# Moving GpSimd's arithmetic to accumulating transfers, TensorE and VectorE in a two-layer decoder trunk

## Chip, cores and metric

The program runs on one core of a Trainium2 chip. The metric is the device time of one execution in microseconds; the time before is the median of three runs. Five engines work side by side and meet at semaphores: TensorE (PE, with its weight loads PEld), VectorE (DVE), ScalarE (ACT), GpSimd (POOL) and SyncE (SP). SP issues plain transfers. POOL issues the transfers that add to what lies at their destination; these appear in the trace as DMA_DIRECT2D on POOL, and their packets as the software_dynamic queue.

## What is computed

A hidden state of 528 tokens (16 learned ones and 512 of the input) by 1024 channels, held transposed as eight tiles `h[m]` of 128 channels x 528 tokens, goes through two layers.

- Layer 0, mixer: RMS norm, one input projection to q, k, v, forget gates and a gated convolution branch. Eight heads of causal attention with forget gates run beside a causal depthwise convolution of width 31 over 4 x 128 channels (`u[i]` in, `cv[i]` out), a layer norm over these 512 channels and SiLU. One output projection maps both back, and the result is added to `h`.
- Layer 1, mixer: causal mean pooling with windows 2, 4, 8 and 16 over four groups of channels, each mean less the channel itself, then a 256 x 256 product for each group, scaled and added to `h`.
- After each mixer a gated MLP: RMS norm, up-projection to 2 x 2816, causal depthwise convolution of width 3, SiLU(gate) x value, down-projection, residual.
- A final RMS norm; the 16 learned tokens are dropped.

## The kernel before

**Weights.** Every 128 x 128 weight tile is used in two float32r parts: a rounded part `wH` and the rest `wL`. Activations are split into `xH`, `xL` likewise, and a product is three matmuls (`xH wH`, `xL wH`, `xH wL`) of 264 columns for each half of the tokens. Weights arrive in chunks of eight tiles (512 KB). `prepare(c)` loads a chunk (SP, `raw<-wts`), rounds it to `wH` (L224 on ACT, or L225 on DVE for the 20 numbers in `VECTOR_CHUNKS`), writes `-wH` into `wL` (L178, ACT) and lets POOL issue a transfer that adds `raw` to it (L179). Three chunks are in flight up to the first MLP, then four. A projection tile of 128 outputs in layer 0's mixer uses exactly one chunk.

**Order.** Matmuls are in the order written in the program: `first_products` (gates and the first tile, k by k as `h` arrives), 7 more tiles of the convolution branch, and then `PE_ORDER`, in which `F` is half of a q, k or v tile, `MA0` to `B13` are steps of the four pairs of heads, `O` is half an output tile, and SUM, MEAN, VAR and SILU are the layer norm's steps. In the pooling, DVE's order is written out as well, in `POOL_ORDER`: `Z` scales by the norm's factor R, `S` makes the window sums, `T` corrects the first 16 tokens, `D` forms the result and adds it to `h`, `X` splits `h` into `xH`, `xL` and issues the matmuls of four up-projection tiles for this k, `Q` squares for the next norm. All other instructions are placed by a planner that simulates the program; each engine then runs its own list strictly in order.

**The 31 convolution taps.** When `u[i]` is complete, `done_g` puts its taps into two lists. Kind 0 is one DVE instruction per tap (L495). Kind 1 is a product on ACT (L498, two buffers) and an addition on POOL (L499). `fill(pace)` takes from the lists after every half tile, by the amounts in `PACE`; `ln_sum` (SUM) takes the rest.

**Sums of squares.** `squares(m, apart)` squares `h[m]` on ACT (L247) and adds it to `acc` on POOL (L249); the last `apart` tiles go to the matmul with ones by themselves. Five norms use it: before layer 0's mixer (`APART[0]`, while `h` arrives), after the output projection, in the second half of each down-projection, and in the pooling.

**Other work on POOL.** Clearing constants (`late`, held behind the first norm's sums), `u x sigmoid` (L479), the layer norm's sums (L758, L768, L787), some casts of q and k (`COPIES`, letter P), small casts (L414, L622, L720), the gates' sum (L529), three of the `Z` (`POOL_Z`, L1013), six of the additions to `h` in `D` (`POOL_RES`, L1037), and six of the sixteen last output tiles (L1092).

Of the kernel before, what the change touches and what calls it, by code (L numbers as in the profile page):

```python
# [20 lines left out]
KT = 8  # L21
# [38 lines left out]
POOL_CHUNKS = (6, 7, 8, 10, 13, 14, 15, 16, 17, 18, 19, 20, 21, 22, 23, 24, 25, 28, 31, 34, 97, 98, 100, 101, 102, 104, 105, 106, 107)  # L60
# [18 lines left out]
POOL_RES = (1, 2, 3, 4, 5, 7)  # L79
POOL_Z = (1, 4, 6)  # L80
# [15 lines left out]
COPIES = ('AAAAA', 'VAAAV', 'APAAA', 'PAPAV')  # L96

VECTOR_CHUNKS = (2, 3, 6, 9, 10, 14, 26, 27, 29, 30, 31, 33, 34, 96, 100, 101, 102, 105, 106, 107)

WARM = 12  # L100

TAPS3 = 3
# [25 lines left out]
def trunk_kernel(  # L128
# [41 lines left out]
    def prepare(c):  # L170
# [69 lines left out]
    def squares(m, apart, t0=0, t1=T, part=True):  # L240
# [5 lines left out]
        sq = wk.tile([P, T], F32, tag="sq", name=f"sq{m}")  # L246
# [57 lines left out]
    with ExitStack() as mx:  # L304
# [31 lines left out]
        for m in range(KT):  # L336
            i_ = squares(m, APART[0], part=SPLIT_FIRST)
            if SQ_AFTER[m] is not None:
                after(i_, xs_[SQ_AFTER[m]])
        ident = pt[:, C_ID:C_ID + P]  # L340
# [47 lines left out]
        def late(ap, x):  # L388
            after(nc.gpsimd.memset(ap, x), state["sum"])

        def constants():
# [19 lines left out]
            for tri, to in ((upper, maskU), (lower, maskL)):  # L411
                late(to[:, P:P + NMETA], 0.0)
                for c0 in (0, P + NMETA):
                    after(nc.gpsimd.tensor_copy(to[:, c0:c0 + P], tri), state["sum"])  # L414
# [53 lines left out]
        def done_g(i):  # L468
            t_ = wk.tile([P, T], F32, tag="sq", name=f"sg{i}")

            def fn(hf, ps):
# [18 lines left out]
        def tap(i, j, kind):  # L490
# [18 lines left out]
        def first_products():  # L509
# [5 lines left out]
            ws = [next_weight(("in", "a", 0, k)) for k in range(KT)]  # L515
            for k in range(KT):
# [12 lines left out]
            nc.gpsimd.tensor_tensor(cell["f"], cell["f"], low, op=ALU.add)  # L529
# [71 lines left out]
        def attention(p):  # L601
# [6 lines left out]
            def values():  # L608
# [13 lines left out]
                nc.gpsimd.tensor_copy(hv2, hv.bitcast(F32))  # L622
# [59 lines left out]
            def scores(hh):  # L682
                tl = st[hh]
                for x, parts in enumerate(BL):
# [34 lines left out]
                    if x == 3:  # L719
                        nc.gpsimd.tensor_copy(P4[hh][64:80, :], ph.bitcast(F32))  # L720
# [35 lines left out]
        def sum_of(x, y, name):  # L756
            t_ = wk.tile([P, T], F32, tag="sq", name=name)
            nc.gpsimd.tensor_tensor(t_, x, y, op=ALU.add)  # L758
            return t_

        def ln_sum():
# [6 lines left out]
            nc.gpsimd.tensor_tensor(a1, a1, a2, op=ALU.add)  # L768
# [4 lines left out]
        def ln_mean():  # L773
# [5 lines left out]
            for i in range(NCONV):  # L779
# [6 lines left out]
                else:  # L786
                    nc.gpsimd.tensor_tensor(cell["var"], cell["var"], s_, op=ALU.add)  # L787

        def ln_var():
            rs = wk.tile([P, T], F32, tag="sq", name="rstd")  # L790
# [39 lines left out]
        with tc.manual_schedule(engines={mybir.EngineType.PE}):  # L830
# [3 lines left out]
            first_products()  # L834
            for n_, unit in enumerate([lambda: None, *in_units(GLU_ORDER[1:])], 1):
                unit()
                if n_ == NORM_AT:
                    cell["R"] = inv_rms([sp(f"ssq{x}")[:, :TH] for x in range(2)], 0)
# [151 lines left out]
    with ExitStack() as px:  # L990
# [19 lines left out]
        def scale_z(m):  # L1010
            if m >= POOL_HALF:
                eng = nc.gpsimd if m in POOL_Z else nc.vector
# [183 lines left out]
```

## Time and profile before

| | |
|---|---|
| median of 3 runs | 1095.64 us (1095.36 to 1096.54) |
| profiled execution | 1095.61 us, span of its trace 1093.5 us, so 2.1 us outside the span |
| PE busy | 1037.5 us, 95% of the span, 8356 matmuls |
| DVE busy | 586.6 us, 54%, 868 instructions |
| ACT busy | 622.4 us, 57%, 872 instructions |
| POOL busy | 306.1 us, 28%, 397 instructions |

Busy time of PE counts matmuls that overlap in a pipeline, so 95% busy is not PE at its peak rate; the count of matmuls in a stretch says more. The chain of waits is the work that ended last, followed back from the end. Windows give busy time of each engine in a stretch, the clock granted to TensorE (1.00 is the upper of its two levels, 2.4 GHz), the mean busy share of the 16 DMA engines, and what they moved. PE, DVE, ACT and POOL are as above; a trailing q is the engine's queue of issues.

### The profile page before, as it was taken

To read this page: it belongs to the slowest core of one execution; us is meant where nothing else is said; L and a number is where in the kernel's file an instruction comes from. 1 tells how busy PE (TensorE), PEld (TensorE's weight loads), DVE (VectorE), ACT (ScalarE), POOL (GpSimd) and SP (SyncE) were. 2 spreads that over 40 slices of the span, in tenths; PEclk is the share of its full clock that TensorE was granted. 3 is DMA by queue.
4 is the path that set the end of the run, shared out by engine and by line. 5 is a ranking of instruction groups with operands and counts; after the bars stand their busy time and mean duration, and the time that the engine had idled before them with its cause. 6 is when DMAs were issued, how large, how long until landed. Compare 5 with 4: busy or idle time off the path is not lost.

```text
span 1093.5 us, 20138 instructions
## 1 busy us (share of the span) xinstructions
PE 1037.5 (95%) x8356; PEld 1023.8 (94%) x8356; DVE 586.6 (54%) x868; ACT 622.4 (57%) x872; POOL 306.1 (28%) x397
## 2 busy tenths in 40 slices
PE   7988789999999999999999998789999999999996
PEld 6978689999999999999999998789999999999995
DVE  5799999886318741024454225927853015545213
ACT  6647656786448753345556657346755335655642
POOL 7666552323311111111111134531111111111222
PEclk9998899999999999999999999899999999999998
DMA  6755333536987778777888777458778878878762
GB/s 215 187 142 132 83 74 99 157 79 159 220 199 170 178 171 186 184 174 178 187 181 178 184 174 174 111 120 192 176 174 193 191 164 192 184 176 198 170 135 77
DMA packets 51995, 178.18 MB, mean 163 GB/s; under 512 B 6208, under 2 KB 8256, under 8 KB 51904
## 3 DMA queue, kind: packets, MB, share of 16 engines
q0 software_dynamic: 23840, 84.98, 42.7%
q1 hardware_dynamic: 26720, 90.68, 25.9%
q8 instruction: 66, 1.08, 0.4%
q10 hardware_dynamic: 1344, 1.23, 0.3%
q14 instruction: 25, 0.20, 0.1%
HBM read 89.80 MB, written 2.10 MB: 84 GB/s over the span
## 4 chain that ended last, share of the span: by engine, by line
PE 78%; DVE 13%; ACT 3%; issue 2%; DMA 2%; POOL 1%; DVEq 0%; SPq 0%; POOLq 0%; ACTq 0%
PE up L198 44%; PE dn L198 23%; DVE h L495 5%; PE wo L198 3%; PE ps_v L198 1%; PE ps_a L198 1%; PE s L198 1%; PE o L198 1%; DVE xL L260 1%; DVE N L660 1%; DVE ws L1023 1%; DVE PL L718 1%; PE ps_k L198 1%; DMA raw<-wts 1%; DVE ws L1035 1%
## 5 line engine op out<-in xcount | busy, mean ns | idle before, releaser
L179 POOL DMA_DIRECT2D wL<-raw x162 | 138.1, 852 | 644.5 <-ACT wL L178 609.6
L198 PE MATMUL up<-xL,wH 128*128 128x264 f32 (+1 forms) x1408 | 288.0, 286 | 13.5 <-DVE xL L260 13.5
L198 PE MATMUL up<-xH,wH 128*128 128x264 f32 (+1 forms) x1408 | 287.1, 285 | 1.9 <-ACT xH L259 1.9
L198 PE MATMUL up<-xH,wL 128*128 128x264 f32 (+1 forms) x1408 | 287.3, 286 | 0.0
L224 ACT CAST wH<-raw 128x1024 fp32r<-128x1024 f32 x142 | 149.0, 1050 | 220.6 <-PE up L198 110.7
L198 PEld LDWEIGHTS up<-xL,wH 128*128 128x128 f32 x1408 | 220.3, 191 | 15.0 <-DVE xL L260 15.0
L198 PEld LDWEIGHTS up<-xH,wH 128*128 128x128 f32 x1408 | 220.5, 190 | 2.5 <-ACT xH L259 2.5
L198 PEld LDWEIGHTS up<-xH,wL 128*128 128x128 f32 x1408 | 219.8, 191 | 0.2 <-DMA wL<-raw 0.2
L178 ACT ACTIVATE wL<-wH 128x1024 fp32r<-128x1024 f32 x162 | 170.5, 1052 | 40.0 <-DVE wH L225 17.2
L923 DVE SCALAR_TENSOR_TENSOR t<-u,par,t 128x528 f32<-128x528 f32 (+1 forms) x176 | 131.0, 759 | 57.1 <-ACT t L920 54.1
L198 PE MATMUL dn<-gH,wH 128*128 128x264 f32 (+1 forms) x704 | 146.1, 284 | 0.0
L198 PE MATMUL dn<-gL,wH 128*128 128x264 f32 (+1 forms) x704 | 145.9, 283 | 0.0
L198 PE MATMUL dn<-gH,wL 128*128 128x264 f32 (+1 forms) x704 | 145.6, 283 | 0.0
L974 DVE TENSOR_TENSOR h<-dn,h 128x528 f32<-128x528 f32 (+1 forms) x30 | 21.0, 700 | 176.0 <-PE dn L198 176.0
L198 PEld LDWEIGHTS dn<-gL,wH 128*128 128x128 f32 x704 | 110.4, 189 | 0.1
L198 PEld LDWEIGHTS dn<-gH,wH 128*128 128x128 f32 x704 | 110.2, 189 | 0.1
L198 PEld LDWEIGHTS dn<-gH,wL 128*128 128x128 f32 x704 | 109.8, 188 | 0.0
L953 DVE TENSOR_TENSOR u<-up,R 128x528 f32<-128x528 f32 (+1 forms) x74 | 51.7, 701 | 104.7 <-PE up L198 104.6
L495 DVE SCALAR_TENSOR_TENSOR h<-u,par,h 128x528 f32<-128x528 f32 x88 | 86.8, 999 | 0.9
L920 ACT ACTIVATE t<-u,par 128x528 f32<-128x528 f32 (+1 forms) x88 | 70.9, 820 | 2.0 <-DVE u L960 2.0
L249 POOL TENSOR_TENSOR acc<-acc,sq 128x528 f32<-128x528 f32 (+1 forms) x30 | 45.3, 1508 | 34.6 <-ACT sq L247 34.3
L499 POOL TENSOR_TENSOR h<-h,tap 128x528 f32<-128x528 f32 x32 | 49.4, 1543 | 11.1 <-ACT tap L498 9.9
(248 smaller groups left out, 1573.9 us busy)
## 6 DMA issues: line engine op xcount, KB each, us to landing
raw<-wts SPq DMA_DIRECT2D x162, 512.0 KB, 4.3
wL<-raw POOLq DMA_DIRECT2D x162, 512.0 KB, 5.8
h<-hT SPq DMA_DIRECT2D x8, 264.0 KB, 6.0
hm<-hT SPq DMA_DIRECT2D x8, 264.0 KB, 7.0
outT<-y ACTq DMA_DIRECT2D x1, 512.0 KB, 3.1
outT<-y SPq DMA_DIRECT2D x1, 512.0 KB, 3.9
par<-par SPq DMA_DIRECT2D x1, 476.5 KB, 6.6
outT<-y ACTq DMA_DIRECT2D x1, 384.0 KB, 2.8
```

The costliest lines, as they stand in the source:

```text
L178: nc.scalar.mul(wL, wH.bitcast(F32), -1.0)
L179: nc.gpsimd.dma_start(wL, raw, accum_op=ALU.add)
L198: nc.tensor.matmul(out, lhsT, rhs, start=start, stop=stop)
L224: return nc.scalar.copy(out, src)
L249: state["sum"] = nc.gpsimd.tensor_tensor(acc[:, t0:t1], acc[:, t0:t1], sq[:, t0:t1], op=ALU.add)
L260: nc.vector.scalar_tensor_tensor(xL[m][:, t0:], h[m][:, t0:], col(gcol + m), xH[m][:, t0:].bitcast(F32), op0=ALU.mult, op1=ALU.subtract)
L495: nc.vector.scalar_tensor_tensor(cv[i], src, cw(i, j), cv[i], op0=ALU.mult, op1=ALU.add)
L499: nc.gpsimd.tensor_tensor(cv[i], cv[i], pr, op=ALU.add)
L920: nc.scalar.activation(t_, uu[:, off + 2:off + 2 + nt], AF.Identity, scale=col(c0 + 2), bias=col(c0 + 3))
L923: nc.vector.scalar_tensor_tensor(t_, uu[:, off + x:off + x + nt], col(c0 + x), t_, op0=ALU.mult, op1=ALU.add)
L953: nc.vector.tensor_tensor(v2(ud), ps[:, :, :nu], v2(R[:, tu:tu + 2 * nu]), op=ALU.mult)
L974: nc.vector.tensor_tensor(v2(h[m][:, td:]), ps[:, :, :nd], v2(h[m][:, td:]), op=ALU.add)
```

## The change

GpSimd keeps its transfers, its clearing of constants, one tiny product of parameters and the last output tiles; the rest of its arithmetic goes elsewhere.

- Taps: all 31 of channel tile 1 become kind 1, the other three tiles kind 0 (90 on DVE instead of 88, 30 on ACT instead of 32, the first of each tile on ACT as before). Kind 1 adds the product by an accumulating transfer of 264 KB instead of POOL arithmetic. `PACE` changes.
- Sums of squares: the first norm's squares go one by one to matmuls with ones inside `first_products` (16 float32 matmuls); in the other four norms `acc` grows by accumulating transfers (25).
- Pooling: all `Z` on DVE; `D` of tiles 1 to 5 adds to `h` by an accumulating transfer, tiles 0, 6 and 7 on DVE; a new `POOL_ORDER`.
- Chunks: all rounding on ACT; of the first three chunks the rest `wL` is a DVE subtraction instead of ACT and a transfer.
- `u x sigmoid`, the layer norm's sums and the gates' sum go to DVE; q and k casts to ACT and one to DVE; small casts to ACT. The buffers of squares go from 2 to 3, and the scratch for the descriptors of POOL's transfers is set to 8192.

```diff
-POOL_RES = (1, 2, 3, 4, 5, 7)
-POOL_Z = (1, 4, 6)
+POOL_RES = (1, 2, 3, 4, 5)
-POOL_ORDER = ("Z0 Z1 S0 T1 D0 S1 Z2 T0 Z3 X0 S3 S2 D1 T2 T3 D2 X1 D3 Q0 Z4 Z5 S4 S5 X2 T4 T5 D4 Z6 X3 D5 Z7 "
-              "S6 X4 Q2 Q5 Q1 S7 T7 T6 X5 D6 D7 X6 Q4 Q3 Q6 X7 Q7")
-PACE = ((0.75, 0.25), (3.75, 5.0), (2.5, 4.5), (5.25, 1.25), (4.0, 1.0), (3.25, 3.0))
+POOL_ORDER = ("Z0 S0 D0 Z1 X0 S1 D1 Z2 S2 T2 D2 Z3 S3 Q0 X1 T3 D3 Z4 S4 Q1 X2 T4 D4 Z5 S5 Q2 X3 T5 D5 "
+              "Z6 S6 Q3 X4 T6 D6 Z7 S7 Q4 X5 T7 D7 Q5 X6 X7 Q6 Q7")
+ADDED = 1
+PACE = ((1.0, 0.4), (3.5, 1.4), (3.5, 1.4), (3.5, 1.4), (3.5, 1.4), (3.5, 3.0))
-COPIES = ('AAAAA', 'VAAAV', 'APAAA', 'PAPAV')
-VECTOR_CHUNKS = (2, 3, 6, 9, 10, 14, 26, ...)
+COPIES = ('AAAAA', 'VAAAV', 'AAAAA', 'AAVAV')
+FIRST_CHUNKS = 3
...
-        copy("V" if c in VECTOR_CHUNKS else "A", wH, raw)
-        nc.scalar.mul(wL, wH.bitcast(F32), -1.0)
-        nc.gpsimd.dma_start(wL, raw, accum_op=ALU.add)
+        nc.scalar.copy(wH, raw)
+        if c < FIRST_CHUNKS:
+            nc.vector.tensor_tensor(wL, raw, wH.bitcast(F32), op=ALU.subtract)
+        else:
+            nc.scalar.mul(wL, wH.bitcast(F32), -1.0)
+            nc.gpsimd.dma_start(wL, raw, accum_op=ALU.add)
...
-            state["sum"] = nc.gpsimd.tensor_tensor(acc[:, t0:t1], acc[:, t0:t1], sq[:, t0:t1], op=ALU.add)
+            nc.gpsimd.dma_start(acc[:, t0:t1], sq[:, t0:t1], accum_op=ALU.add)
...
-            after(nc.gpsimd.memset(ap, x), state["sum"])
+            nc.gpsimd.memset(ap, x)
...
-                    nc.gpsimd.tensor_tensor(uu, uu, t_, op=ALU.mult)
+                    nc.vector.tensor_tensor(uu, uu, t_, op=ALU.mult)
-                        queue[i % 2 if i < 3 or j < TAPS3 else 0].append((i, j))
+                        queue[int(i == ADDED)].append((i, j))
...
-                nc.gpsimd.tensor_tensor(cv[i], cv[i], pr, op=ALU.add)
+                nc.gpsimd.dma_start(cv[i], pr, accum_op=ALU.add)
...
             for k in range(KT):
+                sq = first_square(k)
                 for x in (xH, xL):
...
+                square_sums(sums, 0, [sq], k == 0, k == KT - 1)
...
-            eng = nc.gpsimd if m in POOL_RES else nc.vector
-            eng.tensor_tensor(h[m], h[m], s_, op=ALU.add)
+            if m in POOL_RES:
+                nc.gpsimd.dma_start(h[m], s_, accum_op=ALU.add)
+            else:
+                nc.vector.tensor_tensor(h[m], h[m], s_, op=ALU.add)
```

## Rows read from the trace of the kernel before

**Rows 1.** Windows: stretch, PE, PEld, DVE, ACT, POOL busy (count), clock, DMA share, GB/s.

```profile
0.00:26.00 26.00, 19.81 (x117) 17.72 (x117) 14.89 (x16) 17.65 (x32) 18.50 (x38) 0.93 0.72 225
...
52.00:160.00 108.00, 87.87 (x644) 83.74 (x643) 105.54 (x145) 67.14 (x112) 68.02 (x57) 0.90 0.46 111
160.00:218.00 58.00, 56.79 (x460) 54.30 (x459) 51.27 (x106) 36.52 (x85) 17.44 (x24) 0.98 0.49 128
...
251.00:278.00 27.00, 26.73 (x218) 26.52 (x218) 17.32 (x26) 14.54 (x20) 11.56 (x11) 1.00 0.71 162
...
293.00:296.00 3.00, 3.00 (x27) 3.00 (x26) 0.00 (x0) 0.07 (x1) 0.85 (x1) 1.00 1.08 213
...
603.00:667.00 64.00, 64.00 (x528) 64.00 (x527) 19.45 (x22) 36.52 (x46) 17.55 (x20) 1.00 0.78 180
667.00:723.00 56.00, 41.66 (x290) 39.65 (x289) 45.72 (x46) 28.45 (x44) 31.72 (x31) 0.91 0.53 123
```

**Rows 2.** Chain that ended last, two pieces: start us, us, what.

```profile
83.78 3.84 DVE h L495 x3
...
321.30 87.99 PE up L198 x720
```

**Rows 3.** Timeline of DVE: start us, us, line, operation, out<-in, shape, count.

```profile
60.29 5.21 DVE L495 SCALAR_TENSOR_TENSOR h<-u,par,h 128x528 f32<-128x528 f32 x3
...
175.89 0.75 DVE L495 SCALAR_TENSOR_TENSOR h<-u,par,h 128x528 f32<-128x528 f32 x1
...
705.91 1.25 DVE L1023 TENSOR_TENSOR_SCAN ws<-z 128x528 f32<-128x528 f32 x1
```

**Rows 4.** Timeline of POOL.

```profile
29.97 0.88 POOL L179 DMA_DIRECT2D wL<-raw  x1
...
63.34 5.07 POOL L499 TENSOR_TENSOR h<-h,tap 128x528 f32<-128x528 f32 x3
...
175.51 0.91 POOL L179 DMA_DIRECT2D wL<-raw  x1 [6.33 <-ACT rec L737]
```

**Rows 5.** DVE's groups, 52 to 218 us: busy us, mean ns | idle before.

```profile
L495 DVE SCALAR_TENSOR_TENSOR h<-u,par,h 128x528 f32<-128x528 f32 x80 | 80.7, 1023 | 0.7
...
L663 DVE CAST E<-N 128x5 fp32r<-128x5 f32 x7 | 5.4, 770 | 0.1
```

**Rows 6.** Groups by shape, whole span.

```profile
L923 DVE SCALAR_TENSOR_TENSOR t<-u,par,t 128x528 f32<-128x528 f32 x88 | 66.2, 768 | 30.0 <-ACT t L920 28.5
...
L216 DVE TENSOR_TENSOR gL<-t,gH 128x528 fp32r<-128x528 f32 x22 | 15.6, 708 | 13.6 <-ACT gH L215 13.6
```

**Rows 7.** Tile wL, 72 to 204 us: the issues (ns min/median/max) and landings.

```profile
L179 POOL DMA_DIRECT2D wL<-raw x12: 846/878/914, 72.5 to 196.0; - x12
...
DMA to landing us min/median/max: 4.5/4.6/5.0
```

**Rows 8.** Tile k, 120 to 180 us: landings of 2 KB transfers from POOL.

```profile
DMA to landing us min/median/max: 1.6/2.5/4.5
```

**Rows 9.** DMA queues: packets, MB, time of the packets as a share of 16 engines.

```profile
q0 software_dynamic: 23840, 84.98, 42.7%
q1 hardware_dynamic: 26720, 90.68, 25.9%
```

**Rows 10.** DVE's groups in the pooling, 667 to 720 us.

```profile
L260 DVE SCALAR_TENSOR_TENSOR xL<-h,par,xH 128x528 fp32r<-128x528 f32 x9 | 11.5, 1279 | 3.3 <-ACT xH L259 3.3
L1023 DVE TENSOR_TENSOR_SCAN ws<-z 128x528 f32<-128x528 f32 x6 | 10.6, 1792 | 0.0
L1035 DVE SCALAR_TENSOR_TENSOR ws<-z,ws 128x528 f32<-128x528 f32 x6 | 7.9, 1323 | 0.0
...
L225 DVE CAST wH<-raw 128x1024 fp32r<-128x1024 f32 x3 | 4.3, 1429 | 0.0
```

**Rows 11.** Timeline of PE: first matmul of the second tile, third tile's wait.

```profile
25.92 0.48 PE L198 MATMUL ps_g<-xH,wH 128*128 128x264 f32 x1
...
34.56 0.39 PE L198 MATMUL ps_a<-xH,wL 128*128 128x264 f32 x1 [1.64 <-DMA wL<-raw]
```

More of the change, by code (lines that the diff above doesn't have):

```diff
@@ L245, in squares @@
             return nc.scalar.activation(acc[:, t0:t1], h[m][:, t0:t1], AF.Square)
-        sq = wk.tile([P, T], F32, tag="sq", name=f"sq{m}")
+        sq = wk.tile([P, T], F32, tag="sq", name=f"sq{m}", bufs=3)
         i_ = nc.scalar.activation(sq[:, t0:t1], h[m][:, t0:t1], AF.Square)
         if m < KT - apart:
-            state["sum"] = nc.gpsimd.tensor_tensor(acc[:, t0:t1], acc[:, t0:t1], sq[:, t0:t1], op=ALU.add)
+            nc.gpsimd.dma_start(acc[:, t0:t1], sq[:, t0:t1], accum_op=ALU.add)
             if m == KT - apart - 1 and part:
@@ L335, in trunk_kernel, with first_square @@
         state["emitted"] = 3
-        for m in range(KT):
-            i_ = squares(m, APART[0], part=SPLIT_FIRST)
+        def first_square(m):
+            sq = wk.tile([P, T], F32, tag="sq", name=f"sq{m}", bufs=3)
+            i_ = nc.scalar.activation(sq, h[m], AF.Square)
             if SQ_AFTER[m] is not None:
                 after(i_, xs_[SQ_AFTER[m]])
+            return sq
         ident = pt[:, C_ID:C_ID + P]
@@ L413, in constants @@
                 for c0 in (0, P + NMETA):
-                    after(nc.gpsimd.tensor_copy(to[:, c0:c0 + P], tri), state["sum"])
+                    nc.scalar.copy(to[:, c0:c0 + P], tri)
         H8 = slice(0, HEADS)
@@ L468, in done_g @@
         def done_g(i):
-            t_ = wk.tile([P, T], F32, tag="sq", name=f"sg{i}")
+            t_ = wk.tile([P, T], F32, tag="sq", name=f"sg{i}", bufs=3)
             def fn(hf, ps):
@@ L515, in first_products @@
             ws = [next_weight(("in", "a", 0, k)) for k in range(KT)]
+            sums = [sp(f"ssq{x}")[:, :TH] for x in range(2)]
             for k in range(KT):
+                sq = first_square(k)
                 for x in (xH, xL):
@@ L528, in first_products @@
                 nc.scalar.copy(low[:, half(hf)], ps[32:40, :])
-            nc.gpsimd.tensor_tensor(cell["f"], cell["f"], low, op=ALU.add)
+            nc.vector.tensor_tensor(cell["f"], cell["f"], low, op=ALU.add)
+            return sums
         def gate_sums():
@@ L756, in sum_of @@
         def sum_of(x, y, name):
-            t_ = wk.tile([P, T], F32, tag="sq", name=name)
-            nc.gpsimd.tensor_tensor(t_, x, y, op=ALU.add)
+            t_ = wk.tile([P, T], F32, tag="sq", name=name, bufs=3)
+            nc.vector.tensor_tensor(t_, x, y, op=ALU.add)
             return t_
@@ L786, in ln_mean @@
                 else:
-                    nc.gpsimd.tensor_tensor(cell["var"], cell["var"], s_, op=ALU.add)
+                    nc.vector.tensor_tensor(cell["var"], cell["var"], s_, op=ALU.add)
         def ln_var():
-            rs = wk.tile([P, T], F32, tag="sq", name="rstd")
+            rs = wk.tile([P, T], F32, tag="sq", name="rstd", bufs=3)
             rsqrt(rs, channel_mean(cell["var"], "var"), 1.0 / (P * NCONV), eps[:, 1:2])
@@ L833, in trunk_kernel @@
                 mm(clock[:, :P], ones, ones, True, True)
-            first_products()
+            sums = first_products()
             for n_, unit in enumerate([lambda: None, *in_units(GLU_ORDER[1:])], 1):
@@ L837, in trunk_kernel @@
                 if n_ == NORM_AT:
-                    cell["R"] = inv_rms([sp(f"ssq{x}")[:, :TH] for x in range(2)], 0)
+                    cell["R"] = wk.tile([P, T], F32, tag="R", name="R", bufs=1)
+                    rsqrt(cell["R"], sums, 1.0 / D, eps[:, 0:1])
                     for fn, hf, ps in pending:
@@ L1011, in scale_z @@
             if m >= POOL_HALF:
-                eng = nc.gpsimd if m in POOL_Z else nc.vector
-                eng.tensor_tensor(z[m][:, 16:], z[m][:, 16:], R, op=ALU.mult)
+                nc.vector.tensor_tensor(z[m][:, 16:], z[m][:, 16:], R, op=ALU.mult)
         def window(m):
```

11 lines of the change are left out of this document (4 added, 7 removed).

## The prediction

> **What bounds the kernel now.** I read the chain of waits first. It is PE almost everywhere, at a rate that one long piece gives: 720 matmuls in 87.99 us, 0.122 us each. From about 50 to 160 us it runs through the DVE taps of L495 instead [rows 2]. The windows say how much could be won there [rows 1]. Count times 0.122 is what PE needs: 0 to 26 us 14.3 us (11.7 lost), 52 to 160 us 78.7 (29.3 lost), 160 to 218 us 56.2 of 58, the last stretch of a down-projection nothing, the pooling (667 to 723) 35.4 of 56 (20.6 lost). So all that can be won, about 62 us, lies in three places; the MLPs give nothing.
>
> In 52 to 160 us DVE is busy 105.5 of 108 us, so it is the bound. But its time is inflated. A tap takes 0.75 us while POOL issues a transfer (175.89 and 175.51 [rows 3, 4]), yet three take 5.21 us, 1.74 each, while POOL adds tiles of its own. The groups say the same: L495 means 1023 ns there, while the same instruction form on the same shape means 768 in the MLPs [rows 5, 6]. A cast of five columns means 770 ns. In the pooling, the subtraction for xL, the scans and L1035 are at 1279, 1792 and 1323 ns [rows 10]; alone, a scan takes 1.25 us [rows 3] and the others are of the 768 ns form. POOL's arithmetic holds up VectorE; its issues don't.
>
> **The change, part by part.**
>
> Start. The third tile waits for its wL until 34.56 [rows 11], which POOL issued only at 29.97, behind clearings and the norm's sums [rows 4]. With wL of the first three chunks from DVE (1024 columns, about 1.4 us by scaling the 708 ns of 528 [rows 6]) that wait goes. The second tile could begin as before (25.92) or, if the norm's matmuls and DVE's faster splits fit into the time in which `h` arrives, near 20. The third follows 48 x 0.122 = 5.9 us later, at 26 to 31.8: a gain of 2.8 to 8.6. I take 7.5, near the high end, since 11.7 us of PE's time are lost there, and the 16 new matmuls, even at twice 0.122, are 4 us inside it. The rest of the gain has to be carried on by the weights: chunks land 4.6 us after issue [rows 7], and a chunk feeds 5.9 us of PE with three in flight, so I let it carry.
>
> Attention, 52 to 160 us. VectorE sheds (1023 - 768) x 80 = 20.4 us on taps and most of the 5.4 of the small casts [rows 5], 25 in all. Nearly all of it lies before 160 us, where POOL is busy 68 us against 17 after [rows 1]. It gets three products with sigmoids, three sums of the layer norm, two taps: 8 x 0.71 = 6. DVE's need falls to 86 us. ScalarE has 67 us and gets three roundings and some small casts, about seven instructions at its mean of 622.4 / 872 = 0.71 us: 72. PE needs 79.
>
> The price is in the transfers. No row shows a 264 KB accumulation. The software queue, nearly all of it wL, took 42.7% of 1093.5 us for 84.98 MB [rows 9]: 5.5 us a MB, 2.9 for 512 KB. That fits the landings: 4.5 us for 512 KB, 1.6 for 2 KB [rows 7, 8]. For 0.27 MB it is 1.49 us of all 16 engines, and 3.1 us to landing. From below it could cost what the other queue's bytes cost (25.9% for 90.68 MB), 0.84; from above as much as a whole wL, 2.9, if it goes by rows of 128 partitions and not by bytes. I take 1.49, since wL is the nearest row, the same kind of transfer.
>
> The 30 additions to `cv[1]` are serial, each waiting for the landing before it: 30 x 3.1 = 93 us. They begin after four tiles, about 44 us, and end near 137; at 4.6 each, near 182. The layer norm that needs all of them stands late in the stretch to 218 us, so the chain itself does not set the end. But it sits in POOL's queue: an addition that waits holds the wL issue behind it by up to 3 us, and ACT's products, having two buffers, hold the roundings and exponentials behind them. The engines' time matters more: 0.46 x 108 = 49.7 us of share in this stretch, plus 30 x 1.49 = 44.7, makes 94; the highest share in a window that I asked for is 1.08 [rows 1], so 87 us at least.
>
> VectorE at 86, transfers at 87, PE at 79, ACT at 72: four resources that now wait for one another. I take 91, 5% above the highest, so -17.
>
> The Trainium skill prices a POOL-issued transfer at about 2.0 us plus bytes over 436 GB/s (DMA: Bandwidth & Descriptors, "Anatomy of one DMA"). For 512 KB that is 3.2 us, where the trace has 4.5, so plain transfers are meant and an accumulation is dearer. By the page one addition would be 2.6 us, 0.6 of it bytes, and the stretch would be left to VectorE and PE, at 86 or less.
>
> Layer norm and output, 160 to 286 us. PE is at its rate, so sums at 0.71 on DVE instead of POOL win nothing. In the output projection seven additions join a share of 0.71: 19.2 + 10.4 = 29.6 us in 27, 27.4 at 1.08. In the down-projection before the pooling six join 0.78 x 64 = 49.9: 58.8 of 64. There the last sum must be ready within the 8 us of the last tile (66 matmuls). Residual, square and the two halves of the split at 0.71 each and 3.1 to land make 5.9, if nothing else is in the way. I charge +1.5 for both and for the first chunks after them; if the cover fails, a late weight costs up to its 4.6 us at either place.
>
> Pooling, 667 to 723 us. VectorE: xL 8 x (1.279 - 0.768) = 4.1, scans 6 x (1.792 - 1.25) = 3.3, L1035 6 x (1.323 - 0.768) = 3.3 and three roundings 4.3 go; three Z at 0.71 come: 45.7 becomes 33. PE needs 35. Transfers: 0.53 x 56 = 29.7 plus 5 for `h` and 7 for `acc`, 12 x 1.49 = 17.9, makes 47.6, 44 at 1.08. In the new order h of tile m has the next Z, S, X, T, D, Z, S before its X, some 5 us by the same prices, against 3.1 + 0.7 for ACT's part: covered, with one microsecond to spare. The new wait stands on POOL: each `acc` addition waits for the one before, and later `h` additions and wL issues queue behind it. I take 46, so -10.
>
> Other parts at nothing: clearings and casts moved early (POOL then idle), rounding of the other chunks on ACT (57% busy over the span), the smaller scratch (unless issues grow beyond the 0.91 us of rows 7).
>
> Sum on the profiled execution: 1095.6 - 7.5 - 17 + 1.5 - 10 = 1062.6. Its time is within 0.03 us of the median of the runs. **Forecast 1062 us.**
>
> **Rivals.**
>
> *Transfers cheap, PE the bound.* If an addition costs 0.84 us of the engines, the attention's share is (49.7 + 25.2) / 1.08 = 69 and the pooling's 37. Then the first runs near 82 (PE at the 97% it has after 160 us) and the second near 38: -7.5 - 26 - 18 = 1044. The skill's figure would give this. For it: PE's efficiency in 160 to 218 us. Against: wL's landings.
>
> *Held by in-order queues.* The additions wait on POOL and ACT in another order than the planner thought, so weights and exponentials come late: the attention wins 4, the pooling 5; -7.5 - 4 - 5 + 1.5 = 1081. For it: ACT's busy share in the stretch grows from 62 to 79%, and POOL runs 30 links of one chain. Against: lists are made by readiness, and DVE was the engine that the planner had misjudged.
>
> *Slower: the additions fill the DMA engines.* One mechanism, the engine time x of one addition. With the same 5% and 2 us of loss, attention and pooling take (79.4 + 42x) / 1.08 + 6 instead of 164, so with -6 for start and rest the sign turns at x = 2.4 us. At 2.9, as much as a whole wL, it is (79.4 + 122) / 1.08 + 6 - 164 - 6 = +22: 1118. Against: landings grow with bytes [rows 7, 8].
>
> *It doesn't relieve VectorE.* POOL's issues would hold up DVE as its arithmetic does; 60 more issues of 0.88 us then eat the gain, leaving the start less lateness: 1092. Against: the tap at 175.89 [rows 3, 4].
>
> **How the numbers follow.** Forecast 46%, cheap transfers 18, in-order queues 24, DMA engines full 9, no relief 3. The first reaches from about 1050 to 1074; the range takes in the cheap transfers and most of the queue's case, 1043 to 1084. What this measurement can tell from no change is about 0.2%, 2.2 us. Faster: the first three and most of the last, 0.89; same 0.03; slower 0.08.
>
> **What would show it.** Right: L495 at 0.76 us throughout; the third tile of PE before 29 us; landings of 264 KB near 3.1 to 4 us; clock 1.00 and share above 0.9 between 50 and 140 us; last xL of the pooling some 10 us sooner after the norm's R. Wrong: landings above 5 us with the share at its ceiling, PE waiting for wL in the attention, `acc` late in the down-projection, or L495 still near 1.0 us.

## The result and the profile after

The changed kernel takes 1109.05 us (median of four runs, 1107.93 to 1114.67) against 1095.58: a ratio of 1.0131, 95% interval 1.0095 to 1.0167. It is slower by 1.3%, outside the range, and the forecast of 1062 was 47 us too low. Its profiled execution is the longest of the four, 1114.67 us with a span of 1112.9, and all rows of after are from it, so they show 5.6 us more than the median.

The span splits at a few matmuls. PE's tile views give them: x count, ns min/median/max, first and last start in us. Of the kernel before:

```profile
L198 PE MATMUL ps_g<-xH,wL x64: 278/285/423, 26.8 to 74.4; 128*128 128x264 f32 x64
L198 PE MATMUL mu<-mu,ones x4: 386/386/387, 216.7 to 217.4; 128*128 128x264 f32 x4
L198 PE MATMUL up<-xH,wH x1408: 276/284/420, 278.0 to 1016.9; 128*128 128x264 f32 x88, 128*128 128x258 f32 x88
L198 PE MATMUL dn<-gH,wH x704: 275/283/470, 409.1 to 1081.4; 128*128 128x264 f32 x88, 128*128 128x256 f32 x88
```

Of the kernel after:

```profile
L199 PE MATMUL ps_g<-xH,wL x64: 281/285/288, 26.8 to 67.1; 128*128 128x264 f32 x64
L199 PE MATMUL mu<-mu,ones x4: 386/386/387, 232.2 to 232.9; 128*128 128x264 f32 x4
L199 PE MATMUL up<-xH,wH x1408: 276/284/584, 294.6 to 1036.6; 128*128 128x264 f32 x88, 128*128 128x258 f32 x88
L199 PE MATMUL dn<-gH,wH x704: 276/282/470, 432.5 to 1101.0; 128*128 128x264 f32 x88, 128*128 128x256 f32 x88
```

The eight tiles of the convolution branch, values `ps_a` and gates `ps_g` in turn, are called the GLU tiles from here on. The last GLU matmul (`ps_g`) comes 7.3 us sooner. From there to the layer norm's mean (`mu`) it is 165.1 us and was 142.3: 22.8 lost. From the mean to the first MLP 1.1 are lost, and from its first up matmul to its first down matmul 137.9 - 131.1 = 6.8. From the first pooling matmul to the sums of squares of the second MLP's norm it is 70.0 us and was 73.8: 3.8 won. The rest is within 0.7 us. These cuts are not the prediction's, which counted the attention from 52 us on, when about three of the eight GLU tiles are still to come. Nearly all that went wrong lies in one stretch.

**The attention.** Windows of after (columns as in [rows 1]):

```profile
52.00:160.00 108.00, 83.45 (x591) 79.91 (x589) 78.46 (x146) 58.57 (x100) 32.57 (x40) 0.84 0.76 158
160.00:218.00 58.00, 47.19 (x368) 45.49 (x369) 33.60 (x79) 36.17 (x80) 10.82 (x15) 0.88 0.46 100
```

Beside [rows 1]: VectorE is no longer full, 78.5 of 108 us, as the change meant it to be; ScalarE is at 58.6, down from 67.1; and yet PE gets through 591 matmuls and not 644. No engine is full and the transfers take a share of 0.76, so something waits for something. The waits from the last GLU matmul to the mean (engine, tile and line <- releaser: us in total, times, longest) name it:

```profile
ACT tap L502 <- DMA h<-tap: 50.9, 23, 3.9
POOL h L503 <- DMA h<-tap: 46.7, 17, 4.0
DVE PL L726 <- ACT P L725: 15.8, 9, 10.4
DVE h L746 <- ACT rec L745: 7.6, 8, 2.3
DVE q L577 <- ACT q L225: 7.6, 3, 3.4
DVE mu L766 <- DMA h<-tap: 3.4, 1, 3.4
```

ACT stands still for 50.9 us until an adding transfer of a tap has landed, and VectorE then waits for what ACT has not done. ACT's timeline shows what queues behind such a wait, here wH and wL of a chunk and the rounding of `q`:

```profile
110.52 0.74 ACT L502 ACTIVATE tap<-u,par 128x528 f32<-128x528 f32 x1 [3.85 <-DMA h<-tap]
111.17 1.04 ACT L174 CAST wH<-raw 128x1024 fp32r<-128x1024 f32 x1
115.26 0.73 ACT L502 ACTIVATE tap<-u,par 128x528 f32<-128x528 f32 x1 [3.05 <-DMA h<-tap]
115.90 1.04 ACT L179 ACTIVATE wL<-wH 128x1024 fp32r<-128x1024 f32 x1
116.85 1.25 ACT L225 CAST q<-h 64x528 fp32r<-64x528 f32 x2
```

The chain of 30 additions is issued from 49.1 us on and its last link lands at 180.1: 131 / 30 = 4.4 us a link. A landing takes 3.9 us on average (3.3 to 6.5), and 0.5 us pass from one landing to the next issue; in all 29 links ACT's product was ready before the landing. The timeline of all engines at its end:

```profile
172.55 0.74 ACT L502 ACTIVATE tap<-u,par 128x528 f32<-128x528 f32 x1 [3.06 <-DMA h<-tap]
...
176.81 0.86 POOL L503 DMA_DIRECT2D h<-tap  x1 [2.96 <-ACT q L225]
...
180.11 0.71 DVE L766 TENSOR_TENSOR mu<-h,h 128x528 f32<-128x528 f32 x1 [3.35 <-DMA h<-tap]
180.85 0.28 DVE L631 TENSOR_TENSOR V<-tw,V 16x128 fp32r<-16x128 f32 x1
181.16 0.71 DVE L766 TENSOR_TENSOR mu<-h,h 128x528 f32<-128x528 f32 x1
181.28 0.69 PE L199 MATMUL s<-q,k 128*128 128x272 f32 x2 [3.88 <-DVE V L631]
```

Here `mu<-h,h` is VectorE's first sum for the layer norm. It waits 3.35 us for the last landing, the correction of the values (L631) stands behind it, and PE's scores behind that. From 181.28 us on the chain of waits runs over PE alone until the mean, 51 us.

**The first MLP and the pooling.** The chain of waits at the end of the output projection and after it (start us, us, what):

```profile
275.83 5.17 DMA acc<-sq
...
281.54 3.34 DMA acc<-sq
...
299.71 7.06 DMA acc<-sq
...
307.84 5.57 DMA wL<-raw
...
313.45 6.66 PE up L199 x40
```

Six additions to `acc` in a row hold a wL issue until 307.84 us, and PE goes on only when that has landed. In the pooling the waits are for `h` (691 to 762 us):

```profile
ACT xH L260 <- DMA h<-ws: 12.7, 5, 3.8
PE up L199 <- ACT xH L260: 8.0, 3, 3.9
```

**What an addition takes.** From the page of after (group: count | busy, mean | idle; queue: packets, MB, share; issues: KB each, median us to landing):

```profile
L499 DVE SCALAR_TENSOR_TENSOR h<-u,par,h 128x528 f32<-128x528 f32 x90 | 66.3, 760 | 1.0 <-ACT h L497 0.4
...
q0 software_dynamic: 32048, 99.59, 50.2%
...
h<-tap POOLq DMA_DIRECT2D x30, 264.0 KB, 3.4
acc<-sq POOLq DMA_DIRECT2D x20, 264.0 KB, 4.6
...
h<-ws POOLq DMA_DIRECT2D x5, 264.0 KB, 6.4
```

A lone addition, issued at 132.2 us, in a window of its landing; the 82 GB/s are its own 264 KB:

```profile
132.20:135.50 3.30, 3.30 (x22) 3.30 (x22) 2.07 (x5) 2.18 (x9) 0.90 (x1) 0.72 0.46 82
```

0.46 of the DMA engines for 3.3 us is 1.52 us of all 16: the 1.49 of the prediction. The taps mean 760 ns: the relief of VectorE came as forecast. Both prices were right for an addition alone, and the time still went the other way.

### The profile page after: what moved, and what is told of

It is laid out like the page before. It is cut to its first block, busy times and chain, and to the rows that moved or that the text cites. A ratio compares the mean times of both kernels' runs of the same rounds, so it can differ in the third digit from the quotient of the medians.

```text
span 1112.9 us, 20182 instructions
## 1 busy us (share of the span) xinstructions
PE 1047.5 (94%) x8376; PEld 1033.8 (93%) x8376; DVE 519.8 (47%) x869; ACT 643.9 (58%) x906; POOL 223.2 (20%) x350
## 4 chain that ended last, share of the span: by engine, by line
PE 69%; DMA 8%; issue 3%; ACT 2%; DVE 2%; POOL 1%; DVEq 0%; POOLq 0%; ACTq 0%
PE up L199 44%; PE dn L199 18%; DMA acc<-sq 6%; PE ps_v L199 1%; PE pl L199 1%; PE ps_k L199 1%; DMA h<-tap 1%; PE s L199 1%; PE o L199 1%; PE wo L199 1%; PE m L199 1%; DMA h<-ws 1%; PE ps_q L199 1%; DMA wL<-raw 1%; POOL wL L180 0%
## 5 line engine op out<-in xcount | busy, mean ns | idle before, releaser
L174 ACT CAST wH<-raw 128x1024 fp32r<-128x1024 f32 x162 | 169.8, 1048 | 238.5 <-PE up L199 123.6
L179 ACT ACTIVATE wL<-wH 128x1024 fp32r<-128x1024 f32 x159 | 167.3, 1052 | 1.9
L499 DVE SCALAR_TENSOR_TENSOR h<-u,par,h 128x528 f32<-128x528 f32 x90 | 66.3, 760 | 1.0 <-ACT h L497 0.4
L502 ACT ACTIVATE tap<-u,par 128x528 f32<-128x528 f32 x30 | 22.0, 735 | 53.0 <-DMA h<-tap 52.9
L216 ACT CAST gH<-t 128x528 fp32r<-128x528 f32 (+1 forms) x44 | 27.4, 624 | 43.5 <-DVE t L943 43.3
```

Source lines behind the costliest of these rows:

```text
L174: nc.scalar.copy(wH, raw)
L216: nc.scalar.copy(oH, src)
L499: nc.vector.scalar_tensor_tensor(cv[i], src, cw(i, j), cv[i], op0=ALU.mult, op1=ALU.add)
```

## The experiments

Each run's ratio is to the kernel before on the same chip, whose medians were 1094.5 to 1096.5 us, so a microsecond or two between runs of different chips means nothing. The stretches are from the profiled executions: the last GLU matmul's start, from there to the mean, first up to first down matmul of the first MLP, pooling, all in us.

| run | time (median) | ratio to before, 95% | GLU end | to mean | MLP | pooling |
|---|---|---|---|---|---|---|
| before | 1095.6 | 1 | 74.4 | 142.3 | 131.1 | 73.8 |
| after | 1109.05 | 1.0131 (1.0095 to 1.0167) | 67.1 | 165.1 | 137.9 | 70.0 |
| e1, taps on VectorE | 1086.78 | 0.9913 (0.9893 to 0.9932) | 63.5 | 139.8 | 139.9 | 68.1 |
| e2, five tap buffers | 1106.16 | 1.0082 (1.0058 to 1.0106) | 63.6 | 162.9 | 136.2 | 65.5 |
| e3, `acc` on GpSimd | 1101.91 | 1.0055 (1.0038 to 1.0072) | 63.6 | 164.9 | 129.9 | 67.8 |
| e4, tap sums on GpSimd | 1103.09 | 1.0061 (1.0040 to 1.0081) | 75.2 | 143.3 | 139.9 | 69.8 |
| e5, two chains | 1101.36 | 1.0064 (1.0043 to 1.0086) | 64.4 | 154.2 | 137.9 | 68.6 |
| e6, residuals on VectorE | 1109.74 | 1.0131 (1.0110 to 1.0152) | 65.5 | 164.2 | 137.5 | 69.0 |
| e7, no new transfers | 1073.01 | 0.9802 (0.9785 to 0.9819) | 63.9 | 139.9 | 129.6 | 65.9 |
| e8, e5 with `acc`, `h` on VectorE | 1089.36 | 0.9945 (0.9926 to 0.9964) | 64.0 | 156.1 | 129.5 | 66.0 |
| e9, products alone | 1074.4 | 0.9811 (0.9787 to 0.9836) | 64.4 | 125.7 | 137.7 | 69.5 |
| e10, 16 columns added | 1088.24 | 0.9938 (0.9919 to 0.9957) | 65.5 | 147.6 | 137.6 | 64.9 |
| e11, e7 with ten added | 1081.2 | 0.9869 (0.9841 to 0.9897) | 64.4 | 148.5 | 129.7 | 65.9 |
| e12, e7, first wL by transfer | 1074.6 | 0.9811 (0.9786 to 0.9836) | 66.4 | 139.6 | 129.6 | 65.9 |
| e13, ten in a tile of their own | 1074.66 | 0.9813 (0.9796 to 0.9831) | 63.9 | 141.0 | 129.6 | 66.0 |
| e14, the same, early | 1074.44 | 0.9804 (0.9787 to 0.9821) | 64.4 | 141.2 | 129.6 | 66.0 |

The pooling varies by 5 us between runs in which it has the same code (64.9 to 70.0), so only larger differences there count.

**e1: all taps on VectorE.**

```
-ADDED = 1
+ADDED = -1
```

`PACE` becomes 1.4 and then 4.9 VectorE taps a unit.

> Edit: the changed kernel, but all four channel tiles' taps by VectorE; no product of a tap on ACT, no adding transfer for a tap (30 of each go); the pace of VectorE's taps is raised by 4/3 (1.4 and 4.9). Measured so far: before 1095.6, after 1109.05; from the last matmul of the GLU tiles to the layer norm's mean 142.3 us before and 165.1 after. Theory 1 (ACT's products, having two buffers, wait for the landing of the addition two before and hold ACT's whole list, and VectorE waits for ACT): the hold goes, VectorE gets 30 x 0.76 = 23 us more and is the bound again, at 78.5 + 23 = 101 of 52 to 160 us: the stretch falls by 15 to 23 us, time 1086 to 1094. Theory 3 (the chain of 30 landings itself sets the end of the stretch) and theory 4 (the transfers fill the DMA engines) give the same here. Rival (the stretch is late for another reason: the list's order, or the products and roundings that were moved to VectorE and ACT): VectorE's 23 us come on top, time 1115 to 1132.

22 us faster than after and 0.9% faster than before: the additions of the taps are the loss. The attention's row of this run shows VectorE full again, with PE further along than in either kernel:

```profile
52.00:160.00 108.00, 89.36 (x683) 85.89 (x682) 107.02 (x203) 54.82 (x101) 13.18 (x19) 0.91 0.45 109
```

**e2: five buffers for the products.**

```
-                pr = wk.tile([P, T], F32, tag="tapp", name=f"tap{i}_{j}")
+                pr = wk.tile([P, T], F32, tag="tapp", name=f"tap{i}_{j}", bufs=5)
```

> Edit: the changed kernel with five buffers in place of two for the products of the taps; transfers, chain and engines the same. Theory 1 (two buffers make ACT wait): ACT's idle time put down to the additions falls from 50.9 us to under 20, VectorE's waits for ACT with it, the stretch to the layer norm's mean falls by 10 to 23 us, time 1086 to 1099. Theory 2 (POOL's queue: an addition that waits holds the issues of wL behind it), theory 3 (the chain itself sets the end) and theory 4 (DMA engines full): the same transfers in the same order, so time 1105 to 1112.

1106.16: the first theory falls as it was put. ACT's waits for the landings shrank only to 39.9 us, and the stretch only by 2.2: a chain slower than the pace at which ACT's list asks for products fills five buffers too. The first sum still waits for the end of the chain, and longer than in after:

```profile
174.53 0.71 DVE L766 TENSOR_TENSOR mu<-h,h 128x528 f32<-128x528 f32 x1 [7.13 <-DMA h<-tap]
```

**e3: `acc` by GpSimd's arithmetic.**

```
-            nc.gpsimd.dma_start(acc[:, t0:t1], sq[:, t0:t1], accum_op=ALU.add)
+            nc.gpsimd.tensor_tensor(acc[:, t0:t1], acc[:, t0:t1], sq[:, t0:t1], op=ALU.add)
```

> Edit: the changed kernel, but the sums of squares of the three later norms are added up by GpSimd's arithmetic again, as before, and not by adding transfers; nothing else. Theory 2 (at the start of the first MLP POOL's queue holds wL behind additions to acc that wait for one another): from the first up matmul to the first down matmul of layer 0 falls from 137.9 to 131 to 133, and PE's waits for wL there go; the pooling gives back some of its 4 us, since VectorE is slowed there by GpSimd's arithmetic: time 1101 to 1107. Rival (the additions to acc cost nothing, the loss there is the output projection's): time 1107 to 1111, or more by the slower VectorE of the pooling.

As the second theory has it: the MLP's stretch is 129.9 and no longer 137.9, the attention is untouched. In all variants with additions to `acc` by transfer it is 136.2 to 139.9, in all variants without 129.5 to 129.9.

**e4: the tap sums by GpSimd's arithmetic.**

```
-                nc.gpsimd.dma_start(cv[i], pr, accum_op=ALU.add)
+                nc.gpsimd.tensor_tensor(cv[i], cv[i], pr, op=ALU.add)
```

> Edit: the changed kernel, but the 30 additions of tap products to the second channel tile are GpSimd's arithmetic (as before for its 32 taps) and no transfers. Two things change sides: a product's buffer is free after 1.5 us and not after 4.4, and VectorE's taps are slowed again while GpSimd adds (46 us of GpSimd's time, some 25 taps at 1.8 us in place of 0.76, so 20 to 26 us more of VectorE). Theory 1 (the late buffers hold ACT): the stretch to the layer norm's mean is that of before, 140 to 148 us and not 165: time 1085 to 1092. Rival (VectorE's slowing is dearer than ACT's waits): 1100 to 1112.

Both were half right. The stretch is 143.3, and ACT waits for additions only 5.1 us, but VectorE's taps are slow again (40 to 218 us):

```profile
L499 DVE SCALAR_TENSOR_TENSOR h<-u,par,h 128x528 f32<-128x528 f32 x89 | 87.6, 1007 | 0.6
```

That was paid in the GLU tiles, which end at 75.2 us.

**e5: two chains.** `cvb` is a new tile, joined by VectorE ahead of the layer norm's sums.

```
+                if j == 1:
+                    nc.scalar.activation(cvb, src, AF.Copy, scale=cw(i, j))
+                    return
-                pr = wk.tile([P, T], F32, tag="tapp", ...)
+                pr = wk.tile([P, T], F32, tag=("tapp", "tapq")[j % 2], ...)
-                nc.gpsimd.dma_start(cv[i], pr, accum_op=ALU.add)
+                nc.gpsimd.dma_start((cv[i], cvb)[j % 2], pr, accum_op=ALU.add)
```

> Edit: the changed kernel with the added taps of the second channel tile in two chains: even taps are added to its sum, odd taps to a second tile (its first tap written by ACT, the two joined by VectorE before the layer norm's sums), each chain with two product buffers. 29 transfers of 264 KB in place of 30, issued by the same queue; an addition waits for the landing two before and not for the last one. In the trace of the changed kernel the chain of 30 ran from 49.1 to 180.1 us, 4.4 us a link, and the work that waited for its end (VectorE's sum for the layer norm, then the roundings and scores behind it) started PE's unbroken run only at 181 us. Theory 3 (the serial chain is what the attention waits for): two chains need about half, some 70 us, the stretch from the last GLU matmul to the layer norm's mean falls from 165 to 140 to 150, time 1084 to 1096. Theory 4 or 2 (the number of transfers, their engine time or their place in POOL's queue): the stretch stays above 158, time 1100 to 1110.

154.2 lies between the two expectations, the time at the second's. The additions now run from 47.0 to 132.2 us, but with two under way each lands later:

```profile
DMA to landing us min/median/max: 3.3/5.7/7.3
```

So the queue gives 29 additions in 85 us, 2.9 us each, against 4.4 in one chain. ACT still waits 24.3 us for landings.

**e6: the pooling's residual sums on VectorE.**

```
-POOL_RES = (1, 2, 3, 4, 5)
+POOL_RES = ()
```

> Edit: the changed kernel, but all eight residual sums of the pooling are VectorE's (five adding transfers to h go); sums of squares and taps stay transfers. Theory (in the pooling xH waits for the landing of h's addition, 12.7 us of ACT's idle time and 8 of PE's, and the last waits 7.2 us for it): the stretch from the first pooling matmul to the last norm's sums falls from 70 us to 62 to 66, time 1101 to 1105. Rival (the additions to acc and the wL issues queued behind them on POOL set the pooling's pace): it stays at 69 to 71, time 1107 to 1110.

The rival: 69.0, and the time of after. As far as one run in a stretch that varies by 5 us can tell, the waits for `h` that the profile shows there have no price of their own while `acc` and wL queue on POOL.

**e7: none of the new adding transfers.** The edits of e1 and e6 together, with the sums of squares on VectorE:

```
-            nc.gpsimd.dma_start(acc[:, t0:t1], sq[:, t0:t1], accum_op=ALU.add)
+            nc.vector.tensor_tensor(acc[:, t0:t1], acc[:, t0:t1], sq[:, t0:t1], op=ALU.add)
```

> Edit: the changed kernel with none of its new adding transfers: all taps, all sums of squares and all residual sums of the pooling by VectorE; wL's transfers stay. If the losses found one by one add up (taps 22 us of the total in the run without their transfers, acc about 7, residual sums 4 to 8): 1109 - 22 - 7 - 4 to 8 = 1072 to 1078. If VectorE becomes the bound in their place (25 sums of squares at 0.7 us, 30 taps, 5 residuals), what the acc and residual edits bring is lost: 1082 to 1090.

1073.01: the losses add up, and this version beats both kernels, before by 2.0%. What it keeps of the change is the start, GpSimd without arithmetic, the moved casts and roundings, and the pooling's new order.

**e8: two chains for the taps, the rest on VectorE.** The edits of e5, of e6 and of `acc` in e7.

> Edit: the two chains of taps as in the run of that name, with the sums of squares and the residual sums of the pooling by VectorE. If the serial chain was the loss in the attention and not the transfers, this has VectorE 23 us freer there than the kernel without any of the new adding transfers, and is 0 to 12 us faster than it: 1062 to 1078. If the transfers themselves are the loss: 1092 to 1100.

1089.36, between the two expectations and nearer to the second: against e7 the two chains cost 16 us, all in the attention (156.1 against 139.9).

**e9: the products without their additions.** 30 of the second channel tile's 31 taps are missing from its output.

```
-                nc.gpsimd.dma_start(cv[i], pr, accum_op=ALU.add)
```

> Edit: the changed kernel without the 30 adding transfers of the taps: ACT still forms each product, and it is dropped, so 30 of 31 taps of the second channel tile are missing from the output. This keeps ACT's extra work (30 x 0.74 = 22 us) and VectorE's relief, and takes away every wait for a landing. Theory 3 (the waits for the serial landings, through ACT's list, POOL's and the layer norm's sums, are the loss): the stretch from the last GLU matmul to the layer norm's mean, 165 us, falls below the 140 of the run with all taps on VectorE, to 118 to 132: time 1062 to 1080. Rival (ACT's own work or the moved roundings are what holds the attention, or PE's order): it stays at 138 or more, time 1083 to 1110.

125.7 us. With ACT's extra work and without a wait, the attention is 39 us shorter than after and 14 shorter than with all taps on VectorE:

```profile
52.00:160.00 108.00, 99.96 (x800) 96.41 (x799) 99.62 (x199) 78.14 (x147) 17.33 (x25) 0.97 0.52 124
```

PE does 800 matmuls here and did 591, and its granted clock is 0.97 and not 0.84. The additions' bytes are gone with the waits: the DMA engines' share is 0.52 and not 0.76. This run alone doesn't tell the two apart; the next one does in part.

**e10: additions of 16 columns.** The other 512 columns of the second channel tile lack the taps.

```
-                nc.gpsimd.dma_start(cv[i], pr, accum_op=ALU.add)
+                nc.gpsimd.dma_start(cv[i][:, :16], pr[:, :16], accum_op=ALU.add)
```

> Edit: the changed kernel, but each of the 30 additions of a tap moves 16 of the 528 columns (8 KB and not 264), so the other columns of the second channel tile lack these taps. Same count, same chain, same queues; only bytes go. A 2 KB transfer from POOL landed in 2.5 us, so a link would take 2.5 + 1.1 = 3.6 us in place of 4.4 and the chain 108 us in place of 131. If the fixed part of a link is what costs, the stretch of 165 us falls by no more than 12: time 1097 to 1106. If the bytes on the DMA engines are what costs (0.45 of 16 engines for 3.3 us each), it falls as if the additions weren't there: below 142, time under 1090.

147.6, between the two expectations, with a time under 1090: 17.5 us sooner than with all bytes and still 21.9 later than with no addition at all. A landing takes 2.7 us in the median and never less than 2.0; the products still wait 27.3 us. The DMA engines' share is that of e9:

```profile
52.00:160.00 108.00, 86.66 (x626) 82.68 (x626) 89.19 (x171) 67.96 (x116) 36.79 (x45) 0.87 0.52 110
```

So more than half of the price of the chain does not depend on its bytes. Whether the other 17.5 us come of longer links or of the load on the DMA engines is not told apart here.

**e11: e7 with ten taps added by transfer.**

```
-                        queue[int(i == ADDED)].append((i, j))
+                        queue[int(i == ADDED and j < 11)].append((i, j))
```

> Edit: the kernel with none of the new adding transfers (1073.0 us), but 10 of the second channel tile's 30 taps are added by transfer again, spread out (0.5 a unit), 20 stay on VectorE. If the loss is a chain that outruns its time: 10 links x 4.4 = 44 us end long before the layer norm, ACT waits seldom, VectorE (107 of 108 us busy there) is relieved of 10 x 0.76 = 7.6: the stretch of 139.9 falls by 2 to 8, time 1065 to 1072. If each addition costs by itself, by the 25 us that 30 cost: 10 cost 8, less what VectorE gains: time 1073 to 1081.

Slower than e7 by 8 us, at the far end of the second expectation, and the stretch is 148.5. VectorE had the other 20 taps of the same tile, and the two waited for each other: POOL 10.8 us for L499, L499 5.3 us for a landing, the last sum 5.4.

**e12: the first three wL by transfer.** e7, and:

```
-FIRST_CHUNKS = 3
+FIRST_CHUNKS = 0
```

> Edit: the kernel with none of the new adding transfers (1073.0 us), with wL of the first three chunks by adding transfer again and not by VectorE. In five runs with the changed start the last GLU matmul lies at 63.5 to 65.5 us against 74.4 before. If VectorE's wL is what frees the start, as the prediction has it: PE waits for wL before the second and third tile again, 3 to 7 us later, time 1075 to 1080. If the start's gain is the sums of squares on PE and the freed POOL alone: within 1.5 us, 1072 to 1075.

The GLU tiles end 2.5 us later; the time (1073.32 to 1074.78) can't be told from that of e7 (1072.58 to 1075.59). PE's waits there are for VectorE (1.6 us), none for wL.

**e13 and e14: ten taps in a tile of their own.** `cvb` as in e5, one chain, nine additions; the rest as e7.

```
+                        queue[int(i == ADDED and 1 <= j < 11)].append((i, j))
+                nc.gpsimd.dma_start(cvb, pr, accum_op=ALU.add)
```

> Edit: the kernel with none of the new adding transfers (1073.0 us), with taps 1 to 10 of the second channel tile formed by ACT and gathered in a tile of their own (the first written there, nine added by transfer, one sum on VectorE at the end); the other 21 taps on VectorE, spread out (0.5 a unit). In the run with ten added into the tile that VectorE also writes, additions and VectorE's taps waited for each other, so it could not tell a chain's price from that. If a chain that has time costs nothing: VectorE is relieved of 10 x 0.76 - 0.7 = 6.9 us, the stretch of 139.9 falls by 2 to 7, time 1066 to 1072. If an addition costs wherever it stands, since ACT's product, POOL's issue or the last sum waits for a landing: the stretch is 141 to 149, time 1074 to 1082.

> Edit: the same ten taps in a tile of their own, but early and dense (1.4 a unit from the start): nine links x 4.4 to 6 us, from about 44 to 85 or 95 us, while wL of the GLU tiles shares the queue. If only waits near the end of the stretch cost (the last sum, the roundings behind it): the stretch falls below 139.9, time 1065 to 1072. If ACT's waits for a product's buffer cost wherever they stand: 15 to 20 us of ACT's idle time between 45 and 95 us, stretch 141 to 150, time 1074 to 1083.

The two paces gave nearly the same order (the products lie between 45 and 82 us in both), so they are one experiment, not two. The times of both can't be told from that of e7. In e13 VectorE is relieved by 7 us, 100.0 of 108, and still the stretch is 141.0, not under 139.9:

```profile
52.00:160.00 108.00, 89.29 (x673) 85.53 (x672) 100.00 (x191) 56.50 (x102) 20.20 (x27) 0.91 0.57 127
```

Its waits (63 to 215 us):

```profile
ACT tap L507 <- DMA cvb<-tap: 9.2, 5, 3.5
POOL cvb L508 <- DMA cvb<-tap: 7.8, 3, 3.1
```

Nine links that are over before 92 us, long before the layer norm's sums, take back the 7 us they give VectorE. So the waits early in the stretch cost too, not only those at the end of the chain. Where they cost stands in the timeline of e13:

```profile
68.75 0.74 ACT L507 ACTIVATE tap<-u,par 128x528 f32<-128x528 f32 x1 [3.51 <-DMA cvb<-tap]
...
72.76 0.74 ACT L507 ACTIVATE tap<-u,par 128x528 f32<-128x528 f32 x1 [0.93 <-DMA cvb<-tap]
73.40 0.41 ACT L477 ACTIVATE sg<-sg 128x264 f32<-128x264 f32 x1
73.84 0.71 DVE L483 TENSOR_TENSOR u<-u,sg 128x528 f32<-128x528 f32 x1 [4.17 <-ACT sg L477]
```

ACT's sigmoid `sg` for the last `u` stands behind two products that wait, and VectorE stands idle for it. With two shorter waits for ACT behind it (1.45 and 0.88 us) that is 6.5 us of VectorE by 83 us, nearly all of its 7.

## Why the prediction was wrong, step by step

**Start, -7.5.** 7.3 in the profiled execution, 8.9 to 10.9 in the other runs with this start (e4 and e12 aside). The size was about right, the reason only in part. In the profiled execution the third tile starts at 32.36 us and started at 32.52; only the wait until 34.56 [rows 11] went. In the other runs it starts at 28.7 to 30.8, so 3.8 to 5.8 us are won by then. About 5 us more come behind it, up to the last GLU matmul: that is VectorE's relief, which the prediction counted under the attention, from 52 us on. e4, in which GpSimd adds again beside the GLU tiles, ends them 11.7 us later than e1. wL from VectorE brings 2.5 us (e12), and not at the third tile: there e12 doesn't wait for wL either.

**Attention, -17: the step that failed.** The prices held: L499 at 760 ns, an addition at 1.52 us of the engines and 3.3 us to land when alone, VectorE out of the way. With the waits taken out (e9) the stretch is 125.7, and 142.3 - 17 is 125.3; that they agree is partly luck, since e9 takes the additions' bytes out too, and the prediction's 17 has 5 us of the GLU tiles in it. What failed was "the layer norm that needs all of them stands late in the stretch to 218 us, so the chain itself does not set the end", and after it "the engines' time matters more". The chain was sized at 3.1 us a link, one undisturbed landing; a link took 4.4, a landing beside wL's transfers (3.9 on average) and 0.5 to the next issue. It began at 49 us and not at 44, and ended at 180 and not at 137, at the high bound that the prediction had named and set aside. Its end was late for VectorE's first sum, which in VectorE's list stands at 180 us, 37 us before the mean's old place and with the attention's own work behind it. And on the way 23 products held ACT for 50.9 us. The prediction did write that ACT's two buffers hold the exponentials, and priced it at nothing beyond the 5% of loss.

That the end of the chain sets the end of the stretch shows in the runs with all 30 links in one chain and full size. From the last landing to the mean it is 52.1 us in after, 52.0 in e2, 52.4 in e3 and 51.9 in e6, also in e2, where ACT waits 11 us less on the way. Where the chain is shorter, the mean follows later: 60.2 us after the last landing in e10, 86.4 in e5.

Of the prediction's signs, L495 at 0.76 us came, and a landing alone was in its range; a clock of 1.00 and a share above 0.9 did not (0.84 and 0.76).

The dose runs agree: to the mean it is 125.7 with no link, 147.6 at some 3.5 us a link (47.5 to 152.9 for 30), 154.2 with two chains, 165.1 at 4.4. PE lost twice: it stood idle, and the matmuls that it did were slower. 83.45 us for 591 is 0.141 each, against 0.125 in e9, so at e9's rate they would have taken 9.6 us less. The granted clock of 0.84 is a mixture of the two levels, 1.2 and 2.4 GHz. Three windows of after, around a wait of PE that ends at 164.14 us, show both:

```profile
158.74:164.10 5.36, 0.01 (x1) 0.00 (x0) 3.88 (x13) 1.55 (x3) 0.86 (x1) 0.74 0.99 189
164.14:168.20 4.06, 4.06 (x21) 4.01 (x22) 3.17 (x8) 1.36 (x3) 0.86 (x1) 0.50 0.61 158
168.20:172.40 4.20, 4.18 (x38) 3.92 (x37) 3.74 (x8) 1.27 (x3) 0.86 (x1) 1.00 0.39 68
```

PE is idle in the first; in the second it works at 1.2 GHz (0.50) and gets through 21 matmuls, in the third at 2.4 GHz through 38.

The wait between two links can't simply be left out. The Trainium skill says why (DMA: Bandwidth & Descriptors, "Two DMAs through the same engine are not ordered"): two transfers through one queue have no order but the completion semaphore, and the issuing engine is to wait for the first before it issues the dependent one. In the trace of after POOL does wait, 46.7 us in 17 pieces for landings. No run here leaves that wait out, so none shows what the sum would be without it.

**Output projection and first chunks, +1.5.** The projection is 1.1 longer, within what was charged; the late weight behind it cost 6.8, above the 4.6 named for it. "If the cover fails" was the case: each addition to `acc` waits for the one before, and POOL issues wL in order behind them (e3).

**Pooling, -10.** 3.8 in the profiled execution, up to 8.9 in others with the same code; without any of its new transfers 7.8 to 7.9 (e7 and the runs built on it). VectorE's own gains came (a scan 1.26 us, the subtraction for xL 765 ns, where [rows 10] had 1.79 and 1.28). "Covered, with one microsecond to spare" did not hold: an addition to `h` landed in 6.4 us and not 3.1. `acc` and wL share its queue, and without any of the new transfers the stretch is 65.9 (e7); which of them is the cause was not told apart beyond e6.

**The rivals.** "Held by in-order queues" was the mechanism, with its signs: additions wait on POOL and ACT, and weights (in the MLP) and roundings come late. It was priced as an attention that still wins 4 us; it lost 23. Its argument against, that lists are made by readiness, did not help: a list keeps the place that the plan gave a product, and on the chip 23 of 30 were not ready there. The rival that ended slower, the DMA engines full, gave about the time for the wrong reason: the share was 0.76, and an addition took 1.5 us of them and not the 2.4 at which it turns the sign (its own formula gives 2.3). "Transfers cheap" fell with the same 1.5 us, where it needed 0.84, and "it doesn't relieve VectorE" with L499 at 760 ns. That an accumulation is dearer than a plain transfer, as the prediction has it beside 4.5 us for 512 KB, is not shown: plain loads of 512 KB, issued by SP, land in 4.3 us in the median in the trace of before.

What stays open is how the attention's 39 us would divide between ACT's list, POOL's and the late last sum. With all 30 links the end of the chain decides, as the 52 us show, and in e13 early waits cost through ACT's list. No run moves the layer norm's first sum to a later place in VectorE's list, which would test the failed step by itself, and none takes out one of the waits and leaves the others with all 30 links.

## What to carry to other kernels

A chain of dependent transfers is priced per link by the landing, counted from the issue and beside the other transfers under way, plus what passes until the next issue (here 3.9 and 0.5 us), and then by who stands behind each wait in every in-order list, not by the engines' time. Before work is moved off a slow engine onto such a chain, ask what the least version is: here the relief of VectorE came from taking GpSimd's arithmetic away, and VectorE doing the sums itself (e7, 2.0% faster than before) was not beaten by any kernel here that adds taps by transfer; nine links in a tile of their own (e13, e14) came out about even with it. A last reader that seems to stand late must be looked up in its engine's list, with what stands behind it.

## What the runs showed of the hardware

An accumulating transfer of 264 KB within the chip takes 3.3 us to land when alone (3.9 on average beside wL's) and 1.5 us of the 16 DMA engines; of 8 KB still 2.0 us at least (e10). With two chains under way a landing takes 5.7 us in the median (e5), so a second chain raised the rate only from one in 4.4 us to one in 2.9.

VectorE's multiply-add of 128x528 takes 754 to 761 ns on average in all runs in which GpSimd issues transfers and adds no taps, and 1007 in e4, beside its additions of tiles. The Trainium skill has a reason (SBUF — State Buffer, "Who interferes with whom"): the two share one pair of ports, and a VectorE instruction with two inputs in SBUF contends with a GpSimd instruction that reads SBUF. That the mean rises in e4 and in no other run of the changed kernel agrees with it.
